# Linear attention with ReLU features: the first octet's K in one transfer or in two

## The chip, the cores and the metric

The kernel runs on one core of a Trainium2 chip. The core has five engines that matter here: TensorE (PE in the profile, with its weight loads as PEld), VectorE (DVE), ScalarE (ACT), GpSimd (POOL) and SyncE (SP). Data moves between the device memory and the on-chip memory (SBUF) through 16 DMA engines, which all queues share. The metric is the device time of one execution in microseconds, the median of several runs.

## The reference

Inputs Q, K and V have the shape (8, 12, 512, 64) in float32: 96 heads of 512 positions with 64 values each. For each head:

```python
Q_feat = np.maximum(0, Q)
K_feat = np.maximum(0, K)
KV = np.einsum('bhkd,bhkv->bhdv', K_feat, V)
K_sum = np.sum(K_feat, axis=2)
numerator = np.einsum('bhqd,bhdv->bhqv', Q_feat, KV)
denominator = np.einsum('bhqd,bhd->bhq', Q_feat, K_sum)
return numerator / (denominator[:, :, :, None] + 1e-10)
```

Each of the three inputs and the output has 12.58 MB, and every byte of them is moved once.

## The kernel before

**Tiling.** The 96 heads are worked on as 12 octets of 8 heads. One octet of one tensor is 1 MB of float32: 128 partitions with 2048 values (8 KB) each. A partition holds 32 consecutive positions ("rows" in the kernel, RQ = 32) of one head, so 16 partitions make up a head. A half of a partition's row is 16 positions (R = 16), 4 KB.

**Loads.** All loads of octets 1 to 11, and of Q for octet 0, are issued by GpSimd and turn float32 into bfloat16 on the way (`load`, line 171). Octets 0 and 1 are loaded one at a time, later ones two octets per transfer (`load_two`, line 177). The input tiles have six places (NI = 6), and the loads use six semaphore lanes in turn, so a load waits until the load six before it has landed. K and V of octet 0 take another way: SyncE loads them as float32 (line 259) into the first two of the ten output tiles, `o_sb[0]` and `o_sb[1]`, which are not needed for output until octets 8 and 9. SyncE's transfers use three lanes in turn (`lanes`, line 156); its first stores go on in the same turn.

**One octet's work.** For octet i, `step(i)` and the TensorE program (`products`, line 350) do this:

- VectorE makes `kf` from K (`prep_k`, line 182: ReLU and a mask by head, in two slots s), ScalarE and VectorE make `vo` from V (`prep_v`, line 189), and VectorE copies Q (`copy_q`, line 199).
- TensorE transposes Q into `ps_qt` (line 360), ScalarE evacuates it with ReLU (`relu_q`, line 203).
- TensorE accumulates K^T V and the sums of K into `ps_kv` (line 369); the products of the first 16 rows wait for the semaphores a0 and d0, those of the other 16 for d1. ScalarE copies the result to `kvd` (`evac_kv`, line 209).
- TensorE forms the denominators and the numerators (line 354), VectorE takes the reciprocals (line 223), the numerators are copied (line 218) and transposed back (line 378), and VectorE multiplies them into the output tile in two halves j (`norm`, line 234).
- SyncE stores the output tile (`store`, line 241). All stores also wait for the last K load (the key `("k", (NO - 1) % NI)`), so that they come behind the loads.

**What sets the order.** The order of instructions on each engine is written out by hand in `body`, `setup` and `step`. The class `Order` turns keys that an instruction reads and writes into semaphore waits: an instruction waits for the last writer of each key that it reads, and for the writer and the readers of each key that it writes. Before, K and V of octet 0 have one key each, `("o", 0)` and `("o", 1)`. In `setup` (line 287) `prep_k(0, 0)` and `prep_k(0, 1)` each take all 32 rows of K, and then follow the three preparations of V. The halves of the output tiles have keys `("o", i, j)`; for the two tiles that held octet 0's K and V, `norm` also writes the common key `("o", i)`.

Of the kernel before, what the change touches and what calls it, by code (L numbers as in the profile page):

```python
# [96 lines left out]
def kernel(  # L97
# [8 lines left out]
    B, H, S, D = Q.shape  # L106
# [5 lines left out]
    R = S * 4 // P  # L112
# [4 lines left out]
    NI = 6  # L117
# [11 lines left out]
    def view(X, f):  # L129
        return X.rearrange("b h s d -> (b h s d)").rearrange("(n p f) -> n p f", p=P, f=f)  # L130

    Qr, Kr, Vr, Or = [view(X, RQ * D) for X in (Q, K, V, out)]
# [3 lines left out]
    mask = sb.tile([P, 2, 2], fp32, name="mask")  # L136
    mask_h = sb.tile([P, 8, 2], fp32, name="mask_h")
    kf = sb.tile([P, RQ, 2, D], bf16, name="kf")
    vo = sb.tile([P, RQ, 2, D4], bf16, name="vo")
# [7 lines left out]
    rec = sb.tile([P, RQ], fp32, name="rec")  # L147
    ins = {n: sb.tile([P, NI, RQ * D], bf16, name=f"{n}_sb") for n in "qkv"}
    o_sb = [sb.tile([P, RQ, D], fp32, name=f"o_sb{i}") for i in range(NOUT)]
# [10 lines left out]
    def lane(who):  # L160
        turn[who] += 1
        return lanes[who][(turn[who] - 1) % len(lanes[who])]

    do = Order(nc, sems)

    def kv_src(o):
        if o == 0:
            return (o_sb[0], ("o", 0)), (o_sb[1], ("o", 1))
        return [(ins[n][:, o % NI].rearrange("p (r d) -> p r d", d=D), (n, o % NI)) for n in "kv"]

    def load(n, *octets):
        o, i, m = octets[0], octets[0] % NI, len(octets)
        src = {"q": Qr, "k": Kr, "v": Vr}[n][o:o + m].rearrange("n p f -> p n f")
        do.op("pool", lambda e: e.dma_start(out=ins[n][:, i:i + m], in_=src, single_packet=True),  # L174
              writes=[(n, x % NI) for x in octets], dma=lane("pool"))

    def load_two(o):
        load("q", o, o + 1)
        load("k", o, o + 1)
        load("v", o, o + 1)  # L180

    def prep_k(o, s, halves=(0, 1)):
        src, key = kv_src(o)[0]
        rs = slice(R * halves[0], R * halves[-1] + R)
        do.op("dve", lambda e: e.tensor_scalar(kf[:, rs, s, :], src[:, rs], scalar1=0.0, scalar2=mask[:, 0, s:s + 1],  # L185
                                               op0=Alu.max, op1=Alu.mult),
              reads=[key, ("mask", 0)], writes=[("kf", s, j) for j in halves])

    def prep_v(o, t, halves, who, sem=None):
        src, key = kv_src(o)[1]  # L190
        rs = slice(R * halves[0], R * halves[-1] + R)
        to, src, m = vo[:, rs, t, 2:D + 2], src[:, rs], mask[:, 1, t:t + 1]
        if who == "act":
            make = lambda e: e.activation(to, src, Act.Copy, scale=m)  # L194
        else:
            make = lambda e: e.tensor_scalar(to, src, scalar1=m, scalar2=None, op0=Alu.mult)  # L196
        do.op(who, make, reads=[key, ("mask", 1), "vo1"], writes=[("vo", t, j) for j in halves], sem=sem)

    def copy_q(o):
        do.op("dve", lambda e: e.tensor_copy(q2.rearrange("p u f -> p (u f)"), ins["q"][:, o % NI]),  # L200
# [33 lines left out]
    def norm(o, j):  # L234
        i = (o + 2) % NOUT
        rs = slice(16 * j, 16 * j + 16)
        do.op("dve", lambda e: e.tensor_tensor(o_sb[i][:, rs], ps_x[j].rearrange("p (r d) -> p r d", d=D),  # L237
                                               rec[:, rs].unsqueeze(2).to_broadcast([P, 16, D]), op=Alu.mult),
              reads=[("x", j), "rec"], writes=[("o", i, j)] if i > 1 else [("o", i, j), ("o", i)], sem=f"n{j}")

    def store(o):
        i = (o + 2) % NOUT
# [11 lines left out]
    def memset(who, ap, value, key):  # L254
        do.op(who, lambda e: e.memset(ap, value), writes=[key] if isinstance(key, (str, tuple)) else key)  # L255

    def body():
        for c, X in enumerate((Kr, Vr)):
            do.op("sp", lambda e: e.dma_start(out=o_sb[c].rearrange("p r d -> p (r d)"), in_=X[0]),
                  writes=[("o", c)], dma=lane("sp"))  # L260
        load("q", 0)
        memset("pool", ident, 0.0, "ident")
        do.op("pool", lambda e: e.affine_select(out=ident, in_=ident, compare_op=Alu.not_equal, fill=1.0, base=0,
                                                pattern=[[-1, P]], channel_multiplier=1),
              reads=["ident"], writes=["ident"])
        for n in "kqv":
            load(n, 1)
        ones = vo[:, :, :, 1:D4 - 1]
        for c in range(4):
            memset("pool", ones[:, 8 * c:8 * c + 8, :, 0:D + 2:D1], 0.0, "vo1")  # L270
        for h in range(4):
            for c in range(4):
                memset("pool", ones[32 * h:32 * h + 32, 8 * c:8 * c + 8, h % 2, 0:D + 2:D1], 1.0, "vo1")
        for h in range(4):
            for t in range(2):
                memset("pool", mask[32 * h:32 * h + 32, 1, t:t + 1], 1.0 if h % 2 == t else 0.0,
                       [("m", h, t), ("mask", 1)])
        setup()
        load_two(2)
        load_two(4)  # L280
        for o in range(NO + 1):
            step(o)
        for n in lanes["pool"] + lanes["sp"]:
            nc.gpsimd.wait_ge(sems[n], do.count[n])
        nc.gpsimd.drain()

    def setup():
        do.op("dve", lambda e: e.tensor_copy(ident32, ident), reads=["ident"], writes=["ident32"])
        for c in range(2):
            do.op("dve", lambda e: e.tensor_reduce(  # L290
                out=mask_h[:, :, c], in_=ident32.rearrange("p (h b) -> p h b", h=8), op=Alu.add,
                axis=mybir.AxisListType.X), reads=["ident32"], writes=[("mh", c), "mask_h"])
        do.op("dve", lambda e: e.tensor_reduce(
            out=mask[:, 0, :], in_=mask_h[:, :, 0].rearrange("p (a s) -> p s a", s=2), op=Alu.add,
            axis=mybir.AxisListType.X), reads=["mask_h"], writes=[("mask", 0)])
        prep_k(0, 0)
        prep_k(0, 1)
        prep_v(0, 1, (0,), "act", "a0")
        prep_v(0, 0, (0, 1), "dve", "d0")
        prep_v(0, 1, (1,), "dve", "d1")  # L300
        do.op("dve", lambda e: e.memset(kvf.bitcast(fp32)[:, 0:4 * D1], 0.0), writes=KVD, sem="n0")
        do.op("dve", lambda e: e.memset(kvf.bitcast(fp32)[:, 4 * D1:], 0.0), writes=KVD, sem="n1")
        copy_q(0)
        for j in range(2):
            nc.scalar.sem_inc(sems[f"t{j}"], 1)
            do.note("act", "act", (), (), f"t{j}", 1)

    def step(i):
        r = i + 1
        more, last = i + 1 < NO, i == NO  # L310

        if not last:
            do.looped([("q2", r)], ["q2", "ident"], [("pq", 0)])
            do.looped([], ["q2", "ident"], [("pq", 1)])
            relu_q(0)
            relu_q(1)
            do.looped([("a0", r), ("d0", r)], KF[0], PK + ["pd"])
            do.looped([("d1", r)], KF[1], PK + ["pd"])
            evac_kv()
            if more:  # L320
                prep_v(i + 1, 1, (0,), "act", "a0")
                copy_q(i + 1)
                for j in range(2):
                    prep_k(i + 1, 0, (j,))
                    prep_k(i + 1, 1, (j,))
        if i > 0:
            o = i - 1
            do.looped([("t0", r), ("t1", r)], [*OT, "ident32"], [("x", 0)])
            do.looped([], [*OT, "ident32"], [("x", 1)])
            for j in range(2):  # L330
                norm(o, j)
            if i % 2 and i + 6 < NO:
                load_two(i + 5)
                if i + 7 == NO:
                    for x in range(o):
                        store(x)
            if i + 7 >= NO:
                store(o)
        if not last:
            do.looped([("ev", r)], [*QT, *KVD], ["pd"])  # L340
            denominators()
            for j in range(2):
                do.looped([(f"n{j}", r)], [*QT, *KVD], [("x", j)])
            copy_ot(0, "act")
            copy_ot(1, "act" if more else "dve")
            if more:
                prep_v(i + 1, 0, (0, 1), "dve", "d0")
                prep_v(i + 1, 1, (1,), "dve", "d1")
# [48 lines left out]
    with tc.tile_critical(no_gpsimd_drain=True):  # L397
        body()
        products()
# [34 lines left out]
```

## Time and profile before

| | us |
|---|---|
| median of 3 runs | 125.28 |
| lowest and highest run | 125.17 and 125.55 |
| the profiled execution | 125.0 |
| its span, from the first instruction to the last | 123.2 |

| engine | busy us | share of the span |
|---|---|---|
| VectorE | 86.8 | 70% |
| TensorE products | 83.2 | 68% |
| ScalarE | 76.6 | 62% |
| TensorE weight loads | 71.6 | 58% |
| GpSimd | 20.3 | 17% |

The profile's page divides the span into 40 slices and gives the busy share of each engine and of the DMA engines in tenths for each slice (9 is 90% or more). The bytes of a DMA are counted as they are written, so a load that turns float32 into bfloat16 counts half of what it reads. A timeline row gives the start, the time taken, the engine, the line, the operation, output and inputs, shapes and count, and in brackets the idle time of the engine before it with what ended it. A "q" behind an engine's name is its sequencer, which issues DMAs. A DMA's landing is when its completion signal has come from all 16 DMA engines.

### The profile page before, as it was taken

How to read it: one execution, taken by the hardware profiler on the slowest of the kernel's cores; microseconds unless marked ns; L12 is line 12 of the kernel's file. 1: busy time of each engine (PE TensorE's matmuls, PEld its weight loads, DVE VectorE, ACT ScalarE, POOL GpSimd, SP SyncE). 2: the span in 40 equal slices, each digit the busy share in tenths (PEclk: the TensorE clock that was granted, in tenths of full speed). 3: DMA queues.
4: the chain of work that ended last, by engine and by line, in shares of the span. 5: the costliest groups of instructions: out<-in, count | busy, mean ns of one | idle time of the engine just before them, and what ended most of it. 6: DMA issues, size and time to landing. Idle time of an engine off the chain costs nothing.

```text
span 123.2 us, 3416 instructions
## 1 busy us (share of the span) xinstructions
PE 83.2 (68%) x1440; PEld 71.6 (58%) x1440; DVE 86.8 (70%) x149; ACT 76.6 (62%) x108; POOL 20.3 (17%) x53
## 2 busy tenths in 40 slices
PE   0000085893498898989979899797996959929100
PEld 0000074793297695977958689595885948819000
DVE  0252936625969989899898989989899794593400
ACT  0000755991099994999949997799945999630000
POOL 5887922012022021020220000000000000000000
PEclk9999999999779999999999999999999999995955
DMA  2999999999999999999999999999999999999991
GB/s 61 396 311 237 213 213 217 217 214 215 214 213 213 214 215 213 214 213 214 215 215 214 219 214 213 215 213 213 214 309 424 426 428 423 423 426 426 426 431 64
DMA packets 6676, 32.55 MB, mean 264 GB/s; under 512 B 528, under 2 KB 528, under 8 KB 4880
## 3 DMA queue, kind: packets, MB, share of 16 engines
q0 software_dynamic: 4656, 17.83, 71.9%
q1 hardware_dynamic: 2016, 14.68, 28.7%
q14 instruction: 3, 0.02, 0.0%
q8 instruction: 1, 0.02, 0.0%
HBM read 37.75 MB, written 12.58 MB: 409 GB/s over the span
## 4 chain that ended last, share of the span: by engine, by line
DMA 64%; POOL 9%; DVE 6%; PE 6%; ACT 5%; issue 3%; POOLq 0%; DVEq 0%; SPq 0%
DMA v_sb<-in_V_dram 64%; POOL vo L255 5%; PE ps_x L378 4%; DVE o_sb L237 3%; PE ps_kv L369 2%; ACT ot_sb L220 2%; ACT qt L204 1%; POOL q_sb L174 1%; POOL k_sb L174 1%; ACT kvd L212 1%; ACT vo L194 1%; DVE ot_sb L220 1%; DVE den L229 1%; POOL mask L255 1%; DVE own L225 1%
## 5 line engine op out<-in xcount | busy, mean ns | idle before, releaser
L237 DVE TENSOR_TENSOR o_sb<-ps_x,rec 128x1024 f32<-128x1024 f32 x24 | 28.5, 1220 | 6.8 <-PE ps_x L378 5.5
L378 PE MATMUL ps_x<-ident,ot_sb 128*128 128x128 f32 x192 | 25.2, 288 | 1.7 <-DVE ot_sb L220 1.7
L369 PE MATMUL ps_kv<-vo,kf 64*128 64x132 bf16 x768 | 25.3, 221 | 1.1 <-DVE vo L196 0.5
L360 PE MATMUL ps_qt<-ident,q 128*128 128x128 bf16 x192 | 14.4, 235 | 16.8 <-DVE q L200 15.9
L369 PEld LDWEIGHTS ps_kv<-vo,kf 64*128 64x128 bf16 x768 | 23.4, 95 | 3.0 <-issue 2.6
L185 DVE TENSOR_SCALAR kf<-k_sb,mask 128x1024 bf16<-128x1024 bf16 x44 | 19.5, 490 | 7.9 <-PE ps_kv L369 3.9
L204 ACT ACTIVATE qt<-ps_qt 128x1024 bf16<-128x1024 bf16 x24 | 23.5, 1040 | 2.1 <-PE ps_qt L360 2.1
L378 PEld LDWEIGHTS ps_x<-ident,ot_sb 128*128 128x128 f32 x192 | 22.3, 148 | 3.2 <-issue 2.0
L360 PEld LDWEIGHTS ps_qt<-ident,q 128*128 128x128 bf16 x192 | 12.5, 106 | 19.2 <-DVE q L200 15.9
L220 ACT COPY ot_sb<-ps_x 128x1024 f32<-128x1024 f32 x23 | 22.2, 1016 | 1.7 <-PE ps_x L354 1.4
L194 ACT ACTIVATE vo<-v_sb,mask 128x1024 bf16<-128x1024 bf16 x11 | 12.7, 1153 | 13.8 <-DMA v_sb<-in_V_dram 13.6
L212 ACT CAST kvd<-ps_kv 64x260 bf16<-64x260 f32 x48 | 18.0, 375 | 2.6 <-PE ps_kv L369 1.6
L354 PE MATMUL ps_x<-qt,kvd 128*128 128x256 bf16 x96 | 14.7, 280 | 6.6 <-DVE o_sb L237 6.2
L354 PEld LDWEIGHTS ps_x<-qt,kvd 128*128 128x128 bf16 x96 | 7.8, 100 | 10.7 <-DVE o_sb L237 9.4
L196 DVE TENSOR_SCALAR vo<-v_sb,mask 128x2048 bf16<-128x2048 bf16 (+1 forms) x22 | 11.6, 568 | 0.0
L200 DVE COPY q<-q_sb 128x2048 bf16<-128x2048 bf16 x12 | 8.6, 716 | 2.7 <-PE ps_qt L360 2.7
L354 PE MATMUL ps_kv<-kvd,qt 128*128 128x16 bf16 x192 | 7.0, 179 | 5.0 <-ACT kvd L212 5.0
L354 PEld LDWEIGHTS ps_kv<-kvd,qt 128*128 128x128 bf16 x192 | 6.1, 96 | 6.5 <-ACT kvd L212 6.3
L194 ACT ACT_TABLE_LOAD x1 | 1.3, 1283 | 12.4 <-DMA o_sb<-in_V_dram 12.4
L174 POOL DMA_DIRECT2D k_sb<-in_K_dram x6 | 4.8, 796 | 14.2 <-DMA k_sb<-in_K_dram 12.6
L174 POOL DMA_DIRECT2D q_sb<-in_Q_dram x7 | 4.7, 678 | 13.6 <-DVE kf L185 8.3
L174 POOL DMA_DIRECT2D v_sb<-in_V_dram x6 | 4.1, 690 | 14.2 <-DMA v_sb<-in_V_dram 14.2
(20 smaller groups left out, 29.6 us busy)
## 6 DMA issues: line engine op xcount, KB each, us to landing
out_dram<-o_sb SPq DMA_DIRECT2D x12, 1024.0 KB, 14.3
q_sb<-in_Q_dram POOLq DMA_DIRECT2D x5, 1024.0 KB, 29.0
k_sb<-in_K_dram POOLq DMA_DIRECT2D x5, 1024.0 KB, 29.0
v_sb<-in_V_dram POOLq DMA_DIRECT2D x5, 1024.0 KB, 29.1
o_sb<-in_K_dram SPq DMA_DIRECT2D x1, 1024.0 KB, 6.5
o_sb<-in_V_dram SPq DMA_DIRECT2D x1, 1024.0 KB, 10.9
q_sb<-in_Q_dram POOLq DMA_DIRECT2D x2, 512.0 KB, 11.5
k_sb<-in_K_dram POOLq DMA_DIRECT2D x1, 512.0 KB, 11.5
```

What stands on the lines that cost most here:

```text
L174: do.op("pool", lambda e: e.dma_start(out=ins[n][:, i:i + m], in_=src, single_packet=True), writes=[(n, x % NI) for x in octets], dma=lane ...
L185: do.op("dve", lambda e: e.tensor_scalar(kf[:, rs, s, :], src[:, rs], scalar1=0.0, scalar2=mask[:, 0, s:s + 1], op0=Alu.max, op1=Alu.mult) ...
L194: make = lambda e: e.activation(to, src, Act.Copy, scale=m)
L196: make = lambda e: e.tensor_scalar(to, src, scalar1=m, scalar2=None, op0=Alu.mult)
L204: do.op("act", lambda e: e.activation(qt[:, j * (U // 2):(j + 1) * (U // 2)], ps_qt[j], Act.Relu), reads=[("pq", j)], writes=[("qt", j)])
L212: do.op("act", lambda e: e.copy(kvd[64 * c:64 * c + 64, s:8:2, c * D1:c * D1 + D1].rearrange("p (g t) d -> p g t d", t=2), ps_kv[64 * s:64 ...
L220: do.op(who, lambda e: e.copy(to, src) if who == "act" else e.tensor_copy(to, src), reads=[("x", j)], writes=[("ot", j)], sem=f"t{j}")
L237: do.op("dve", lambda e: e.tensor_tensor(o_sb[i][:, rs], ps_x[j].rearrange("p (r d) -> p r d", d=D), rec[:, rs].unsqueeze(2).to_broadcast( ...
L354: return pe.matmul(out_, lhsT, rhs, start=True, stop=True, skip_group_check=True)
L360: x = pe.transpose(ps_qt[u // 8][:, u % 8, :], q2[:, u, :], ident)
L369: x = pe.matmul(ps_kv[:, h, 0:2 * (D + 2)].rearrange("p (t d) -> p t d", t=2), kf[ps, R * g + k, :, :].rearrange("p s d -> p (s d)"), vo[p ...
L378: x = pe.transpose(ps_x[u // 8][:, u % 8 * P:u % 8 * P + P], ot[:, u].rearrange("p h c -> p (h c)"), ident32)
```

## The change

K of octet 0 is loaded by SyncE in two transfers, both from all 128 partitions: the first 4 KB of each 8 KB row, then the second 4 KB. V follows as the third transfer, in one piece as before. Each transfer takes the next of SyncE's three lanes. The keys of the two tiles now go by halves, `("o", c, j)`: the transfer of a half writes that half's key, V's transfer writes both. `prep_k` and `prep_v` read the keys of the halves that they take; since both `prep_k` calls for octet 0 still take all 32 rows, they wait for both transfers. `norm` writes the key of its half alone, for all output tiles.

```diff
-    def kv_src(o):
+    def kv_src(o, c, halves):
         if o == 0:
-            return (o_sb[0], ("o", 0)), (o_sb[1], ("o", 1))
-        return [(ins[n][:, o % NI].rearrange("p (r d) -> p r d", d=D), (n, o % NI)) for n in "kv"]
+            return o_sb[c], [("o", c, j) for j in halves]
+        return ins["kv"[c]][:, o % NI].rearrange("p (r d) -> p r d", d=D), [("kv"[c], o % NI)]
...
     def prep_k(o, s, halves=(0, 1)):
-        src, key = kv_src(o)[0]
+        src, keys = kv_src(o, 0, halves)
...
-              reads=[key, ("mask", 0)], writes=[("kf", s, j) for j in halves])
+              reads=[*keys, ("mask", 0)], writes=[("kf", s, j) for j in halves])
...
     def prep_v(o, t, halves, who, sem=None):
-        src, key = kv_src(o)[1]
+        src, keys = kv_src(o, 1, halves)
...
-        do.op(who, make, reads=[key, ("mask", 1), "vo1"], writes=[("vo", t, j) for j in halves], sem=sem)
+        do.op(who, make, reads=[*keys, ("mask", 1), "vo1"], writes=[("vo", t, j) for j in halves], sem=sem)
...
-              reads=[("x", j), "rec"], writes=[("o", i, j)] if i > 1 else [("o", i, j), ("o", i)], sem=f"n{j}")
+              reads=[("x", j), "rec"], writes=[("o", i, j)], sem=f"n{j}")
...
-        for c, X in enumerate((Kr, Vr)):
-            do.op("sp", lambda e: e.dma_start(out=o_sb[c].rearrange("p r d -> p (r d)"), in_=X[0]),
-                  writes=[("o", c)], dma=lane("sp"))
+        for c, X, halves in ((0, Kr, (0,)), (0, Kr, (1,)), (1, Vr, (0, 1))):
+            rs = slice(R * halves[0], R * halves[-1] + R)
+            do.op("sp", lambda e: e.dma_start(out=o_sb[c][:, rs].rearrange("p r d -> p (r d)"),
+                                              in_=X[0][:, rs.start * D:rs.stop * D]),
+                  writes=[("o", c, j) for j in halves], dma=lane("sp"))
```

## The prediction

> **What bounds the kernel now.** I read the page first: the busy tenths by slice, then the chain that ended last (64% of it is one long DMA entry), then the waits of SyncE, then stages of the span, and only then single rows of the timeline around the first octet and the end.
>
> The page's slices say that the DMA engines are full almost from the first slice to the last, while no other engine is.
>
> ```profile
> span 123.2 us, 3416 instructions
> PE   0000085893498898989979899797996959929100
> DVE  0252936625969989899898989989899794593400
> DMA  2999999999999999999999999999999999999991
> HBM read 37.75 MB, written 12.58 MB: 409 GB/s over the span
> ```
>
> Cut into stages (each row: the stage, its length, busy time of PE, PEld, DVE, ACT and POOL, granted clock, DMA share, GB/s), the same is sharper:
>
> ```profile
> 1.00:3.00 2.00, 0.00 (x0) 0.00 (x0) 0.23 (x1) 0.00 (x0) 1.46 (x4) 1.00 0.37 78
> 3.00:5.50 2.50, 0.00 (x0) 0.00 (x0) 0.74 (x3) 0.00 (x0) 2.27 (x8) 1.00 1.01 419
> 34.00:63.00 29.00, 26.62 (x477) 22.86 (x474) 26.07 (x46) 25.21 (x36) 4.29 (x6) 0.97 1.06 214
> 118.00:120.00 2.00, 0.00 (x0) 0.00 (x0) 0.00 (x0) 0.00 (x0) 0.00 (x0) 0.50 1.02 430
> 121.00:123.20 2.20, 0.00 (x0) 0.00 (x0) 0.00 (x0) 0.00 (x0) 0.00 (x0) 0.50 0.04 15
> ```
>
> From 3 us to 120 us the share is 1.01 or above. The 214 GB/s in the middle counts bf16 as written; those loads read twice that from f32, about 428 GB/s, the same rate as the stores. So 50.33 MB at 430 GB/s is 117.0 us, and the flow runs from about 2.7 to about 120.6, with the slowest DMA engine ending near 121.7. The kernel's time is when the flow starts, plus its bytes, plus a short end.
>
> The compute engines don't set the end. The last store is issued at 115.74, and SyncE then waits 5.6 us for it, behind stores already queued. Before that, compute is itself held by the loads at each pair of octets:
>
> ```profile
> SPq L405 <- DMA out_dram<-o_sb: 5.6, 1, 5.6
> ```
> ```profile
> 33.80 1.15 ACT L194 ACTIVATE vo<-v_sb,mask 128x1024 bf16<-128x1024 bf16 x1 [5.60 <-DMA v_sb<-in_V_dram]
> 77.86 1.15 ACT L194 ACTIVATE vo<-v_sb,mask 128x1024 bf16<-128x1024 bf16 x1 [1.62 <-DMA v_sb<-in_V_dram]
> 93.88 1.15 ACT L194 ACTIVATE vo<-v_sb,mask 128x1024 bf16<-128x1024 bf16 x1 [2.88 <-DMA v_sb<-in_V_dram]
> ```
>
> **The change part by part.** All against the profiled execution, 125.0 us (span 123.2 and 1.8 around it); that lies 0.28 below the median of 125.28, and I add the sum to the median.
>
> *Issue on SyncE.* The two transfers of before:
>
> ```profile
> 0.96 0.39 SPq L259 DMA_DIRECT2D o_sb<-in_K_dram  x1
> 1.40 0.43 SPq L259 DMA_DIRECT2D o_sb<-in_V_dram  x1
> 7.53 2.48 DVE L185 TENSOR_SCALAR kf<-o_sb,mask 128x2048 bf16<-128x2048 f32 x2 [3.70 <-DMA o_sb<-in_K_dram]
> 12.44 1.95 DVE L196 TENSOR_SCALAR vo<-o_sb,mask 128x2048 bf16<-128x2048 f32 x2 [2.43 <-DMA o_sb<-in_V_dram]
> ```
>
> One more issue of about 0.43 puts K's second half at 1.40 and V at 1.84 instead of 1.40. The DMA engines have K to do until about 5.2, and V's first packets need about 1 us from issue (K: issued 0.96, only three packets started before 2.0), so V is ready near 2.9 and the delay costs nothing. SyncE's next instruction is a store at 87.68; nothing else is queued behind.
>
> *Between K's halves.* The first half is 512 KB, 1.2 us at 430 GB/s, so it lasts until 3.9 at least; the second half's packets are ready at about 2.4 by the same lead. 1.5 us of cover: no gap, 0. Without cover it would be a gap of up to the lead, 1.0 us.
>
> *Twice the completions.* GpSimd's loads are each released by a landing. Those of one octet (1 MB) are 2.45 us apart, those of two octets (2 MB) 4.87:
>
> ```profile
> 16.93 0.70 POOL L174 DMA_DIRECT2D k_sb<-in_K_dram  x1 [1.64 <-DMA q_sb<-in_Q_dram]
> 19.38 0.71 POOL L174 DMA_DIRECT2D v_sb<-in_V_dram  x1 [1.75 <-DMA v_sb<-in_V_dram]
> 24.33 0.70 POOL L174 DMA_DIRECT2D q_sb<-in_Q_dram  x1 [4.25 <-DMA q_sb<-in_Q_dram]
> 29.20 0.84 POOL L174 DMA_DIRECT2D k_sb<-in_K_dram  x1 [4.17 <-DMA k_sb<-in_K_dram]
> 34.07 0.77 POOL L174 DMA_DIRECT2D v_sb<-in_V_dram  x1 [4.03 <-DMA v_sb<-in_V_dram]
> ```
>
> Two times 2.45 less 4.87 is 0.03: in a queue that is never empty, cutting the same bytes into two transfers costs at most 0.03 us.
>
> *Half-size packets.* K goes from 128 packets of 8 KB to 256 of 4 KB, 8 more on each DMA engine, all on the bounding resource. No row shows a 4 KB read, so I bound it. From 6 to 9 us the two queues share the engines:
>
> ```profile
> q0 software_dynamic: 78, 0.32, 52.3%
> q1 hardware_dynamic: 78, 0.63, 52.2%
> ```
>
> The 4 KB written by the one took 0.523 x 48 / 78 = 0.322 us, the 8 KB of the other 0.321. Since the first kind reads 8 KB too, this fits a price by bytes read (nothing extra), but also a price by packet: then each added packet costs a full one, 8 x 0.306 (2.45 us for 8 rows) = 2.45 us, the upper end. A third row is nearer. Between 5.0 and 5.5 us SyncE's queue has 33 packets, 78.7% of 8 us = 6.30 us, and 13 of them are the few bytes of a completion; the other 20 at 0.309 make 6.18, so a tiny packet takes 0.009 us. That is the part that doesn't go with bytes, and it speaks for the price by bytes: 8 x 0.009 + 0.009 for the added completion = 0.08 us. I take 0.08, which holds the 0.03 above, and keep 0 and 2.45 as ends. Below 0 only an earlier start of the flow could bring it (a rival).
>
> Here the Trainium skill has a figure. Its page "DMA: Bandwidth & Descriptors", section "iDMA fabric — 4 AXI ports for 8 engines, asymmetric across TPBs", gives 408.7 GB/s for a stream of 1 MiB loads from SyncE with 4 KiB rows; by it K's 1.05 MB would take 2.57 us instead of 2.44, and the sum would be +0.13 instead of +0.08. No run here shows such rows yet.
>
> *Waits and turns.* The K preparation on VectorE still takes all 32 rows, so it waits for both halves: one more wait, on an engine that sits idle 3.70 us there anyway. Of the 16 DMA engines, 15 had finished K by 5.5 us (the small packets: 2 before 5.0, 13 after); the last, held by one 16 KB instruction fetch of 0.93 us, finished about 7. There the queues take packets in turn, so with the packets halved K gets one turn more behind a software packet: K and V on that engine land some 0.32 us later, K near 7.8, V near 12.7. VectorE has 2.43 idle between them; the shift of the first products is swallowed by ScalarE's 5.60 at 33.80. Cost 0; uncovered it would be 0.32. SyncE's semaphore lanes move by one, and the stores that reuse lanes of the first loads find them long landed.
>
> *Keys of the output halves.* Normalisations of octets 8 and 9 no longer write the common key, which made the second half wait for the first on VectorE itself: those pairs (90.45 and 98.23) take 2.48 us, pairs such as 83.07 take 2.35. 0.13 twice is saved on VectorE, while SyncE's stores wait in a full queue: 0 at the end.
>
> Sum: +0.08 us on the path, so 125.0 becomes 125.08 and the median 125.28 becomes 125.36 us, +0.06%.
>
> **The rivals.**
>
> *A half packet costs nearly a whole one* (slower). The place is 2.7 to 5.2 us, the price up to 2.45 us: 127.7 us. It decides from 0.047 us per added packet (8 x 0.047 = 0.38, which is 0.3%). For it: reading every second 4 KB is a pattern that no row shows. Against: the 0.009 us of the tiny packets, and the equal price of all 8 KB reads.
>
> *A gap between the halves* (slower). If the second half's packets are made ready only after the first has run, the engines idle for the lead of 1.0 us: 126.4. For it: before 3 us there are only 19 packets, so the start is slow. Against: later transfers follow without a gap (the 0.03). The Trainium skill, same page, section "Anatomy of one DMA — SWDGE (gpsimd) path", gives each DMA a fixed cost of about 2.0 us; paid in series for one more DMA that would be 127.4, but the trace's 2.45 against 4.87 shows no such cost where the queue is full.
>
> *An earlier start of the flow* (faster). If the time from issue to first packet goes with a transfer's bytes, half of 1.04 us is saved: 125.36 - 0.52 = 124.84. It decides from 0.46 us. For it: in the stage from 1 to 3 us the DMA share is only 0.37. Against: the number of rows per transfer, 128, doesn't change.
>
> *Later first products* (slower). V's landing would have to slip by more than the 5.60 at 33.80 before any of it reaches the end; from 0.32 that is far.
>
> **How the numbers follow.** What a measurement of this kernel can tell from no change is about 0.3%, 0.38 us. The forecast, within that, has 0.60. Dearer packets 0.14, a gap 0.08, later products and what I don't see 0.04: slower 0.26. The earlier start 0.12 and 0.02 unseen: faster 0.14. The time is the likeliest case's, 125.36; its own range is 125.0 to 125.7 (the runs of before spread over 0.38). Stretched to the near part of the rivals, half of the earlier start below and 0.8 us of dearer packets or gap above, the range is 124.8 to 126.1; what lies past it holds no more than 0.2.
>
> **What would show it.** Right: SyncE's queue has 144 packets more; the stage 3 to 5.5 us keeps a share near 1 and 419 GB/s; the K preparation starts between 7.4 and 8.0; the first q_sb load of two octets released by a landing stays within 0.2 us of 24.33, the last store's landing likewise. Wrong: a lower rate in the stage from 3 to 5.5 (packet price), a share under 1 between 3 and 4 (gap), packets well before 2.0 (earlier start), or an end that moves while the landings up to 93.9 don't (compute after all).

## The result, and the profile after

The changed kernel takes 125.80 us (125.73 to 125.94) against 125.36 us (125.15 to 125.55) before: a ratio of 1.0042 with a 95% interval of 1.0032 to 1.0051. That is 0.44 us slower, just past the 0.38 us (0.3%) that the prediction named as the bound of no change. The time lies in the stated range of 124.8 to 126.1, but in the case "slower", which had a chance of 0.26, and not in the likeliest one, whose own range was 125.0 to 125.7.

The page of the changed kernel: span, DMA slices with their rates, SyncE's queue, and the chain that ended last by engine.

```profile
span 123.9 us, 3415 instructions
DMA  2999999999999999999999999999999999999990
GB/s 73 317 317 272 213 213 218 213 214 213 213 216 214 213 218 214 214 212 213 217 216 213 218 214 214 212 213 216 214 320 428 426 423 426 420 423 434 423 415 32
q1 hardware_dynamic: 2160, 14.68, 28.9%
PE 39%; DVE 28%; DMA 14%; POOL 8%; issue 4%; POOLq 0%; DVEq 0%; SPq 0%
```

The DMA engines are as full as before. SyncE's queue has 2160 packets instead of 2016, 144 more, and the same bytes. The chain now goes mostly through TensorE and VectorE, which looks as if compute had become the bound. It hasn't. The last store is issued earlier than before, and SyncE then waits longer for it, 6.8 us instead of 5.6. Before:

```profile
115.74 0.33 SPq L246 DMA_DIRECT2D out_dram<-o_sb  x1
```

After:

```profile
115.33 0.33 SPq L246 DMA_DIRECT2D out_dram<-o_sb  x1
```
```profile
SPq L407 <- DMA out_dram<-o_sb: 6.8, 1, 6.8
```

The issue time differs from one execution to the next without moving the end: in e1 below, which has the transfers of before and its time, the last store is issued at 114.55 us and SyncE waits 7.1 us. So the DMA flow still sets the end, and it runs later. The stages of the changed kernel (columns as in the prediction: busy times of PE, PEld, DVE, ACT, POOL, then clock, DMA share and GB/s) show where:

```profile
1.00:3.00 2.00, 0.00 (x0) 0.00 (x0) 0.23 (x1) 0.00 (x0) 1.46 (x4) 1.00 0.38 94
3.00:5.50 2.50, 0.00 (x0) 0.00 (x0) 0.74 (x3) 0.00 (x0) 2.27 (x8) 1.00 1.03 338
34.00:63.00 29.00, 26.67 (x458) 23.14 (x459) 25.38 (x48) 25.47 (x36) 5.00 (x6) 0.94 1.06 215
118.00:120.00 2.00, 0.00 (x0) 0.00 (x0) 0.00 (x0) 0.00 (x0) 0.00 (x0) 0.50 1.02 430
121.00:123.90 2.90, 0.00 (x0) 0.00 (x0) 0.00 (x0) 0.00 (x0) 0.00 (x0) 0.50 0.06 25
```

The middle and the end have the rates of before. Only the stage from 3 to 5.5 us fell, from 419 to 338 GB/s, and there the DMA share stayed at 1.03: the engines count as busy while they move less. Packets of GpSimd's queue, which count half of what they read, start a little earlier in this stage than before, so part of the 338 is bookkeeping. The single microseconds before they start are clean. Before:

```profile
2.00:3.00 1.00, 0.00 (x0) 0.00 (x0) 0.23 (x1) 0.00 (x0) 0.93 (x4) 1.00 0.57 131
3.00:4.00 1.00, 0.00 (x0) 0.00 (x0) 0.74 (x3) 0.00 (x0) 1.00 (x3) 1.00 0.99 418
4.00:5.00 1.00, 0.00 (x0) 0.00 (x0) 0.00 (x0) 0.00 (x0) 0.89 (x4) 1.00 1.11 459
```

After:

```profile
2.00:3.00 1.00, 0.00 (x0) 0.00 (x0) 0.23 (x1) 0.00 (x0) 0.93 (x4) 1.00 0.66 176
3.00:4.00 1.00, 0.00 (x0) 0.00 (x0) 0.74 (x3) 0.00 (x0) 1.00 (x3) 1.00 1.02 270
4.00:5.00 1.00, 0.00 (x0) 0.00 (x0) 0.00 (x0) 0.00 (x0) 0.89 (x4) 1.00 1.00 389
```

From 3 to 4 us, while K's first halves are being read, 270 GB/s move instead of 418. The runs below in which SyncE's first transfer has whole 8 KB rows in all 128 partitions (e1, e4, e6, e9, e10) have 393 to 410 there, so this row is clear. The row from 2 to 3 us is not: the same runs have 106 to 172, since a packet counts where it starts and 16 engines with one 8 KB packet each are 131 KB. Over the three rows the changed kernel moved 835 KB, before 1008, those runs 917 to 1020; the 82 to 185 KB that are missing are 0.19 to 0.43 us at 430 GB/s. GpSimd's loads, each released by the landing of an earlier one, show the delay further on. The last of them before, and then five of the changed kernel:

```profile
63.49 0.70 POOL L174 DMA_DIRECT2D v_sb<-in_V_dram  x1 [4.24 <-DMA v_sb<-in_V_dram]
```
```profile
17.81 0.70 POOL L174 DMA_DIRECT2D k_sb<-in_K_dram  x1 [1.75 <-DMA q_sb<-in_Q_dram]
20.32 0.73 POOL L174 DMA_DIRECT2D v_sb<-in_V_dram  x1 [1.81 <-DMA v_sb<-in_V_dram]
25.20 0.80 POOL L174 DMA_DIRECT2D q_sb<-in_Q_dram  x1 [4.15 <-DMA q_sb<-in_Q_dram]
30.07 0.71 POOL L174 DMA_DIRECT2D k_sb<-in_K_dram  x1 [4.07 <-DMA k_sb<-in_K_dram]
64.36 0.70 POOL L174 DMA_DIRECT2D v_sb<-in_V_dram  x1 [3.90 <-DMA v_sb<-in_V_dram]
```

Against the rows of before (16.93, 19.38, 24.33, 29.20, and 63.49 for the last) they are 0.88, 0.94, 0.87, 0.87 and 0.87 late. Against the same rows of e1 (17.05, 19.51, 24.46, 29.33, 63.62) it is 0.74 to 0.81. This is more than the 0.44 of the medians: a landing waits for the slowest of the 16 DMA engines, and single executions differ. The span grew by 0.7; of that, 0.3 is that the profiled execution of before lay 0.36 below its median and this one (125.73) only 0.07 below.

That the loss is made at the start and never grows is shown better by bytes. The packets of a trace can be added up in order of their ends, with those of GpSimd's queue counted twice, since it reads twice what it writes. By this count the changed kernel is 0.21 us ahead of before at 0.1 MB, 0.21 behind at 0.5 MB, when K's first half is in, 0.38 behind at 1 MB, and from there 0.31 to 0.43 behind up to 50 MB. Against e1 it is 0.35 ahead, 0.09 behind, 0.24 behind and then 0.22 to 0.33 behind. (That it is ahead at 0.1 MB is in part that a 4 KB packet ends sooner than one of 8 KB.) So the loss is made while K is read, and nothing later adds to it.

The first octet's rows, from the timelines of SyncE and VectorE:

```profile
0.96 0.86 SPq L260 DMA_DIRECT2D o_sb<-in_K_dram  x2
1.87 0.42 SPq L260 DMA_DIRECT2D o_sb<-in_V_dram  x1
8.43 2.48 DVE L185 TENSOR_SCALAR kf<-o_sb,mask 128x2048 bf16<-128x2048 f32 x2 [4.60 <-DMA o_sb<-in_K_dram]
```

The K preparation starts at 8.43 instead of 7.53. On ScalarE the shift is swallowed where the prediction said: its wait for V of octet 2, at 34.69, shrank from 5.60 to 3.77 us and did not vanish.

```profile
34.69 1.16 ACT L194 ACTIVATE vo<-v_sb,mask 128x1024 bf16<-128x1024 bf16 x1 [3.77 <-DMA v_sb<-in_V_dram]
94.76 1.16 ACT L194 ACTIVATE vo<-v_sb,mask 128x1024 bf16<-128x1024 bf16 x1 [2.10 <-DMA v_sb<-in_V_dram]
```

### The profile page after: what moved, and what is told of

The parts are those of the page before. It is cut to its first block, busy times and chain, and to the rows that moved or that the text cites. A ratio compares the mean times of both kernels' runs of the same rounds, so it can differ in the third digit from the quotient of the medians.

```text
span 123.9 us, 3415 instructions
## 1 busy us (share of the span) xinstructions
PE 84.4 (68%) x1440; PEld 73.1 (59%) x1440; DVE 86.3 (70%) x149; ACT 77.2 (62%) x108; POOL 21.2 (17%) x53
## 3 DMA queue, kind: packets, MB, share of 16 engines
q1 hardware_dynamic: 2160, 14.68, 28.9%
## 4 chain that ended last, share of the span: by engine, by line
PE 39%; DVE 28%; DMA 14%; POOL 8%; issue 4%; POOLq 0%; DVEq 0%; SPq 0%
DVE o_sb L237 23%; PE ps_kv L371 17%; DMA k_sb<-in_K_dram 14%; PE ps_x L380 9%; PE ps_qt L362 8%; PE ps_x L356 4%; POOL vo L255 4%; DVE kf L185 2%; POOL q_sb L174 1%; POOL mask L255 1%; DVE ot_sb L220 1%; DVE den L229 1%; DVE own L225 1%; DVE rec L232 1%; DVE vo L196 0%
## 5 line engine op out<-in xcount | busy, mean ns | idle before, releaser
L371 PE MATMUL ps_kv<-vo,kf 64*128 64x132 bf16 x768 | 27.3, 231 | 0.6
L362 PE MATMUL ps_qt<-ident,q 128*128 128x128 bf16 x192 | 15.2, 242 | 17.5 <-DVE q L200 16.6
L371 PEld LDWEIGHTS ps_kv<-vo,kf 64*128 64x128 bf16 x768 | 25.4, 100 | 2.5 <-issue 2.5
L362 PEld LDWEIGHTS ps_qt<-ident,q 128*128 128x128 bf16 x192 | 13.1, 110 | 20.3 <-DVE q L200 16.6
L380 PE MATMUL ps_x<-ident,ot_sb 128*128 128x128 f32 x192 | 23.6, 276 | 1.7 <-DVE ot_sb L220 1.7
L380 PEld LDWEIGHTS ps_x<-ident,ot_sb 128*128 128x128 f32 x192 | 20.8, 140 | 3.2 <-issue 2.0
L194 ACT ACTIVATE vo<-v_sb,mask 128x1024 bf16<-128x1024 bf16 x11 | 12.7, 1154 | 8.9 <-DMA v_sb<-in_V_dram 8.7
L174 POOL DMA_DIRECT2D v_sb<-in_V_dram x6 | 5.1, 850 | 13.8 <-DMA v_sb<-in_V_dram 13.8
L174 POOL DMA_DIRECT2D k_sb<-in_K_dram x6 | 4.6, 765 | 14.2 <-DMA k_sb<-in_K_dram 12.5
```

Source lines behind the costliest of these rows:

```text
L362: x = pe.transpose(ps_qt[u // 8][:, u % 8, :], q2[:, u, :], ident)
L371: x = pe.matmul(ps_kv[:, h, 0:2 * (D + 2)].rearrange("p (t d) -> p t d", t=2), kf[ps, R * g + k, :, :].rearrange("p s d -> p (s d)"), vo[p ...
L380: x = pe.transpose(ps_x[u // 8][:, u % 8 * P:u % 8 * P + P], ot[:, u].rearrange("p h c -> p (h c)"), ident32)
```

## The experiments

All diffs are against the changed kernel. "Row" below is one partition's piece in a transfer. The times at a glance:

| run | SyncE's transfers of octet 0 | us | before, same chip | ratio (95%) |
|---|---|---|---|---|
| changed | K halves, V | 125.80 | 125.36 | 1.0042 (1.0032 to 1.0051) |
| e1 | K, V; new keys | 125.29 | 125.30 | 0.9999 (0.9990 to 1.0008) |
| e2 | V, K halves | 126.07 | 125.30 | 1.0064 (1.0050 to 1.0078) |
| e3 | K as 256 pieces in one, V | 125.68 | 125.30 | 1.0031 (1.0020 to 1.0043) |
| e4 | K, V halves | 125.91 | 125.30 | 1.0055 (1.0041 to 1.0068) |
| e5 | K in contiguous halves, V | 125.07 | 125.38 | 0.9979 (0.9970 to 0.9988) |
| e6 | K, V in contiguous halves | 125.46 | 125.38 | 1.0008 (1.0000 to 1.0017) |
| e7 | K by even and odd partitions, V | 125.71 | 125.38 | 1.0032 (1.0022 to 1.0043) |
| e8 | K; V from ScalarE's queue | 125.44 | 125.38 | 1.0003 (0.9994 to 1.0012) |
| e9 | K, V second halves, V first halves | 125.81 | 125.33 | 1.0035 (1.0022 to 1.0048) |
| e10 | K, V first halves, another octet's second halves | 125.93 | 125.33 | 1.0049 (1.0032 to 1.0066) |
| e11 | K by lower and upper 64 partitions, V | 126.71 | 125.33 | 1.0111 (1.0094 to 1.0128) |
| e12 | K quarters, V | 126.45 | 125.33 | 1.0095 (1.0069 to 1.0122) |

The first theory (S) was that SyncE's queue hands rows to the engines at a limited pace, too slow for small ones; its rivals were a price per small packet (P) and a price per further transfer (B).

**e1, the keys alone.**

```diff
-        for c, X, halves in ((0, Kr, (0,)), (0, Kr, (1,)), (1, Vr, (0, 1))):
+        for c, X, halves in ((0, Kr, (0, 1)), (1, Vr, (0, 1))):
```

> The changed kernel with K in one transfer again; only the keys by halves and their waits stay changed. Theory S (supply): SyncE's queue hands rows to the DMA engines at a limited pace, about 66 rows a microsecond in the stage 3 to 4 us of the changed kernel (270 GB/s of 4 KB rows), and 4 KB rows are drained faster than that, so the engines starve at the start. Theory P (packet price): each added 4 KB packet costs about 0.055 us on its engine (0.44 / 8) wherever it lies. Theory B (boundary): each further transfer in SyncE's queue costs about 0.4 us. All three expect the time of before, 125.36 (125.2 to 125.5), and 418 GB/s from 3 to 4 us. A fourth, that the keys and waits cost the time, expects 125.8.

Measured 125.29 against 125.30. The keys and waits cost nothing and gain nothing; the split is the cause.

**e2, V first, then K's halves.**

```diff
+        for c, X, halves in ((1, Vr, (0, 1)), (0, Kr, (0,)), (0, Kr, (1,))):
```

> The changed kernel with V (8 KB rows) issued first and K's two halves behind it. S: V's rows carry 0.55 MB per us at the same pace, enough for the engines, and K's rows are made ready while V runs: about 125.4 (125.2 to 125.55), 400 GB/s or more from 3 to 4 us. P: 125.8, as many 4 KB packets. B: 125.8, as many transfers. The later K preparation (some 3 us) is expected to be swallowed by ScalarE's wait for V of octet 2 in all three.

Measured 126.07, 0.64% slower, worse than the change itself. S was wrong here: V's rows went at 393 GB/s from 3 to 4 us, near the 400 that it gave, but the loss came all the same, later, when K's halves ran beside GpSimd's queue (the "software queue" from here on, q0 in the profile): from 6 to 9 us 166 packets of both queues started, 217 GB/s, and each software packet took 0.399 us (66.5% of 48 us, which is 3 us of 16 engines, over 80 packets).

**e3, one transfer of 256 pieces of 4 KB.** The second halves go into the third output tile, so that the pieces can't be joined; taken together the transfer reads the whole 1 MB in order.

```diff
+    k_in = o_all[:, 0:4:2, 0:R, :]
...
+        do.op("sp", lambda e: e.dma_start(out=k_in.rearrange("p h r d -> p h (r d)"),
+                                          in_=Kr[0].rearrange("p (h f) -> p h f", h=2)),
+              writes=[("o", 0, 0), ("o", 2, 0)], dma=lane("sp"))
```

> K in a single transfer, but with 4 KB rows: the second halves go to the first half of the third output tile, so that the 256 pieces can't be joined. S: the slow start stays, 125.6 to 125.95, and 250 to 300 GB/s from 3 to 4 us. P: 125.8. B: 125.36, since there is one transfer.

Measured 125.68, in the range that S gave, but not for its reason:

```profile
2.00:3.00 1.00, 0.00 (x0) 0.00 (x0) 0.23 (x1) 0.00 (x0) 0.93 (x4) 1.00 0.51 33
3.00:4.00 1.00, 0.00 (x0) 0.00 (x0) 0.74 (x3) 0.00 (x0) 1.00 (x3) 1.00 0.85 319
4.00:5.00 1.00, 0.00 (x0) 0.00 (x0) 0.00 (x0) 0.00 (x0) 0.89 (x4) 1.00 0.99 401
```

The flow starts later (33 KB from 2 to 3 us, against 106 to 172 with 128 whole rows; its first packet starts at 2.39 us, against 1.99 before), and then 4 KB pieces reach 401 GB/s. Counted in bytes, it is 0.44 us behind before at 0.1 MB and 0.48 at 5 MB. So the one transfer of twice as many rows lost time by a later start; that is another loss than the change's, where the first packet starts at 1.98 and the bytes after it are slow.

**e4, V in halves instead of K.**

```diff
+        for c, X, halves in ((0, Kr, (0, 1)), (1, Vr, (0,)), (1, Vr, (1,))):
```

> K whole (8 KB rows), V in two transfers of 4 KB rows. S: K's rows cover the making of V's; the software queue is there when V's rows fall short, so nothing or little is lost: 125.3 to 125.55, 418 GB/s from 3 to 4 us. P: 125.8. B: 125.8.

Measured 125.91: S fell a second time. From 6 to 9 us, where V's first halves run beside the software queue (q0), and from 10 to 12.5, where the second halves do:

```profile
DMA packets 163, 0.64 MB, mean 214 GB/s; under 512 B 7, under 2 KB 7, under 8 KB 162
...
q0 software_dynamic: 82, 0.34, 71.7%
q1 hardware_dynamic: 81, 0.31, 29.0%
DMA packets 189, 0.71 MB, mean 285 GB/s; under 512 B 15, under 2 KB 15, under 8 KB 189
```

A software packet takes 0.717 x 48 / 82 = 0.420 us in the first window, against 0.322 before. So not only V's halves but also the loads beside them are slowed. The other packets of the first window took (0.290 x 48 - 0.06) / 74 = 0.187 us. That left two theories: the pattern that is read (H), every second 4 KB of device memory, called striped below; and turns between the queues with short packets (T). The next two runs change only which 4 KB pieces a transfer reads.

**e5, K in two transfers, each of a contiguous half.**

```diff
-                                              in_=X[0][:, rs.start * D:rs.stop * D]),
+                                              in_=X[0] if len(halves) == 2 else
+                                              X[0][64 * halves[0]:64 * halves[0] + 64].rearrange("p (y f) -> (p y) f", y=2)),
```

> The changed kernel, but each of K's two transfers reads one contiguous half of octet 0's 1 MB as 128 pieces of 4 KB, instead of every second 4 KB. The writes into SBUF, the sizes, the rows and the transfers stay; K of octet 0 lands in the wrong places, so the first octet's output isn't the reference's. Theory H (pattern read): reading only every second 4 KB of device memory is slow (270 GB/s against 418 from 3 to 4 us), and slows the software queue's loads beside it too; it expects the loss to vanish, 125.2 to 125.45, with 390 GB/s or more from 3 to 4 us. Theory S (supply of rows by SyncE's queue) and every theory that goes by packet size or by the writes expect 125.65 to 125.9 and 270 to 300 GB/s.

Measured 125.07, which is 0.21% (0.12 to 0.30) faster than before, and 0.13 us below the range that H gave. This decides the main question. From 3.2 to 4.8 us, the changed kernel:

```profile
DMA packets 139, 0.52 MB, mean 323 GB/s; under 512 B 16, under 2 KB 16, under 8 KB 138
...
q1 hardware_dynamic: 138, 0.50, 94.3%
```

and e5:

```profile
DMA packets 183, 0.68 MB, mean 425 GB/s; under 512 B 20, under 2 KB 20, under 8 KB 182
...
q1 hardware_dynamic: 178, 0.65, 100.8%
```

With tiny packets at 0.009 us taken out, a 4 KB packet took (0.943 x 25.6 - 0.14) / 122 = 0.197 us in the changed kernel and (1.008 x 25.6 - 0.18) / 158 = 0.162 us in e5. Same size, same count, same places in SBUF, same two transfers; only every second 4 KB became consecutive 4 KB. The 0.197 is a mean of two rates. From 3.2 to 4.0 us, in K's first half, a 4 KB packet of the changed kernel took 0.248 us and one of e5 0.161; from 4.2 to 4.8 us, in the second half, the changed kernel's took 0.161 too. Only the first striped transfer is slow. e5's flow also moves more in its first microsecond:

```profile
2.00:3.00 1.00, 0.00 (x0) 0.00 (x0) 0.23 (x1) 0.00 (x0) 0.92 (x4) 1.00 0.86 270
3.00:4.00 1.00, 0.00 (x0) 0.00 (x0) 0.74 (x3) 0.00 (x0) 1.00 (x3) 1.00 1.06 422
```

270 KB from 2 to 3 us instead of 106 to 172; the 98 to 164 KB more are 0.23 to 0.38 us at 430 GB/s, and 0.31 was gained. Its first packet starts no earlier (2.02 us, against 1.98 in the changed kernel and 1.99 before). It is no kernel to keep as it stands, since K lands in the wrong places; a layout that reads so and lands rightly was not tried.

**e6, V in two contiguous halves.** The edit of e5 on e4.

> The run with V in two transfers, but each of the two reads a contiguous half of octet 0's V as 128 pieces of 4 KB; V of octet 0 lands in the wrong places, so the first octet's output isn't the reference's. There the software queue's packets took 0.420 us each from 6 to 9 us (71.7% of 48 us over 82) instead of 0.322. H: they take 0.32 again and the time is 125.2 to 125.45. Theory T (turns: a packet of the one queue behind a short packet of the other is not fetched in time): they stay at 0.40 to 0.44 and the time at 125.8 to 126.0.

Measured 125.46, the same as before but for 0.17% at most, and 0.01 past the range that H gave. The two windows of e4 again:

```profile
DMA packets 211, 0.80 MB, mean 266 GB/s; under 512 B 16, under 2 KB 16, under 8 KB 211
...
q0 software_dynamic: 106, 0.43, 71.2%
q1 hardware_dynamic: 105, 0.36, 32.6%
DMA packets 183, 0.68 MB, mean 270 GB/s; under 512 B 18, under 2 KB 18, under 8 KB 183
```

A software packet takes 0.712 x 48 / 106 = 0.322 us and one of V's pieces (0.326 x 48 - 0.14) / 89 = 0.174. T is out: here short packets in turns cost nothing when the pieces are consecutive.

**e7, K by even and odd partitions, 8 KB rows.**

```diff
+        for x in range(2):
+            do.op("sp", lambda e: e.dma_start(out=o_sb[0][x::2].rearrange("p r d -> p (r d)"), in_=Kr[0][x::2]),
+                  writes=[("o", 0, x)], dma=lane("sp"))
```

> K in two transfers of 8 KB rows, the even partitions and the odd ones, so 64 rows each; nothing is read by halves. H, S and T: no slow rows, 125.36 or a little less: with one transfer of 256 rows the flow started some 0.45 us later than with 128, so with 64 it may start 0.2 earlier, 125.1 to 125.35. B (each further transfer costs about 0.4): 125.7.

Measured 125.71, as B said and against the others. But its stages show another loss: 66 KB from 2 to 3 us instead of 106 to 172, and then 393 GB/s from 3 to 4. SyncE also took longer to issue the two, 1.19 us against 0.86 in the changed kernel. The flow started later: its first packet starts at 2.32 us, and counted in bytes it is 0.30 us behind before at 0.1 MB and 0.36 at 5 MB. (The row from 4 to 5 us reads only 258 GB/s, but software packets run in it already, and they count half.) e5 and e6, which have as many transfers and no such loss, exclude a fixed price of 0.4 us per transfer.

**e8, V from ScalarE's queue.** K whole from SyncE, V whole from ScalarE, on a lane of its own, at the same time.

> K whole from SyncE as before, V whole from ScalarE's own queue, issued at the same time as K. If the start of the flow (DMA share 0.37 from 1 to 3 us) is held by one queue's making of rows, two queues fill it sooner: up to 0.35 us less, 124.95 to 125.3. If the start is held by something that both queues share, 125.3 to 125.45. V's landing comes earlier or equal in both.

Measured 125.44, no change (0.9994 to 1.0012). Two queues gave 164 KB from 2 to 3 us, no more than single queues gave, and then only 287 GB/s from 3 to 4. So a second queue did not fill the start sooner.

**e9, V's second halves first.** H had two readings: the second 4 KB of each 8 are quick because of where they lie (H1), or because the stretch has been visited (H2).

```diff
+        for c, X, halves in ((0, Kr, (0, 1)), (1, Vr, (1,)), (1, Vr, (0,))):
```

> K whole, V in two transfers of every second 4 KB, but the second halves of the rows first. In the run with the first halves first, only the first of the two transfers was slow: 163 packets of all queues from 6 to 9 us (211 with contiguous halves), 189 from 10 to 12.5 (183 with contiguous halves). Theory H2 (a first visit by halves is slow, the second visit to the same stretch of memory is not): again 155 to 175 packets from 6 to 9 and 180 to 195 from 10 to 12.5, time 125.8 to 126.05. Theory H1 (reading the first 4 KB of 8 is slow, the second 4 KB not): about 205 from 6 to 9 and 140 to 155 from 10 to 12.5.

Measured 125.81, and again the transfer that comes first is the slow one (179 packets in the first window, a little above the range that H2 gave, 183 in the second; with contiguous halves 211 and 183):

```profile
DMA packets 179, 0.70 MB, mean 233 GB/s; under 512 B 9, under 2 KB 9, under 8 KB 178
...
q0 software_dynamic: 89, 0.36, 61.4%
q1 hardware_dynamic: 90, 0.34, 39.6%
DMA packets 183, 0.71 MB, mean 285 GB/s; under 512 B 9, under 2 KB 9, under 8 KB 183
```

H1 is out. But here the software packets of the first window took 0.614 x 48 / 89 = 0.331 us, hardly more than in e6, and V's own pieces (0.396 x 48 - 0.08) / 81 = 0.233 instead of 0.174. So which of the two queues shows the loss is not the same in every run.

**e10, the second halves of another octet.**

```diff
-                                              in_=X[0][:, rs.start * D:rs.stop * D]),
+                                              in_=X[halves == (1,)][:, rs.start * D:rs.stop * D]),
```

> K whole, then the first halves of the rows of V's octet 0, then the second halves of the rows of V's octet 1, 1 MB further on (so half of octet 0's V is another octet's, and the first octet's output isn't the reference's). H2: the second transfer now is a first visit too and as slow as the first: 155 to 175 packets from 6 to 9 us and 140 to 160 from 10 to 12.5, time 126.2 to 126.6. If only the first such transfer of an execution is slow, or only first halves: 180 to 195 from 10 to 12.5, 125.8 to 126.05.

Measured 125.93, with 178 and 187 packets:

```profile
DMA packets 178, 0.69 MB, mean 231 GB/s; under 512 B 9, under 2 KB 9, under 8 KB 178
...
DMA packets 187, 0.70 MB, mean 282 GB/s; under 512 B 15, under 2 KB 15, under 8 KB 187
```

The second transfer reads a stretch that nothing has visited (GpSimd's own load of it starts after 15 us), and is not slow. H2 is out too. What is left is what was seen: in the changed kernel (270, then 389 GB/s) and in e2, e4, e9 and e10, the first striped transfer is slow and the second is not. From 10 to 12.5 us a software packet takes 0.322 us in e2, e4, e6, e9 and e10 alike, and a 4 KB piece 0.170 to 0.172. Why only the first stays open.

**e11, K by lower and upper 64 partitions, 8 KB rows, each transfer contiguous.**

```diff
+        for x in range(2):
+            do.op("sp", lambda e: e.dma_start(out=o_sb[0][64 * x:64 * x + 64].rearrange("p r d -> p (r d)"),
+                                              in_=Kr[0][64 * x:64 * x + 64]),
+                  writes=[("o", 0, x)], dma=lane("sp"))
```

> K in two transfers of 64 partitions each with whole 8 KB rows, so each transfer reads a contiguous 512 KB, and the output is the reference's. Pattern theories (H): nothing is slow, 125.0 to 125.4; the lower end if a transfer of half the bytes starts the flow earlier, as in the run with contiguous halves (270 GB/s from 2 to 3 us against 131 before), the upper end if the split by partitions starts it later, as with even and odd partitions (66). Theory B: 125.7.

Measured 126.71, outside every expectation. From 3.2 to 4.8 us:

```profile
DMA packets 59, 0.37 MB, mean 230 GB/s; under 512 B 10, under 2 KB 10, under 8 KB 20
...
q1 hardware_dynamic: 48, 0.31, 87.0%
```

Of the 48 packets 38 are 8 KB (0.31 MB): (0.870 x 25.6 - 0.09) / 38 = 0.58 us each, nearly twice the 0.309 of before. What e11 has alone is that one transfer writes 64 neighbouring partitions: e5 read the same contiguous 512 KB, and e7 had transfers of 64 whole rows, both without slow packets. The Trainium skill's page "DMA: Bandwidth & Descriptors", section "Rules for kernel authors", advises against two transfers to the two halves of the partitions because they serialize. The advice holds here, but the trace shows more than no gain: while one half of the partitions takes all writes, a packet takes nearly twice as long.

**e12, K in quarters of 2 KB.**

SyncE's lanes are five instead of three here, one for each transfer.

```diff
+        for x in range(4):
+            do.op("sp", lambda e: e.dma_start(out=o_sb[0][:, 8 * x:8 * x + 8].rearrange("p r d -> p (r d)"),
+                                              in_=Kr[0][:, 8 * x * D:(8 * x + 8) * D]),
+                  writes=[("o", 0, x // 2, x % 2)], dma=lane("sp"))
```

> K in four transfers, each of one 2 KB quarter of every 8 KB row. H2: the first quarter reads 0.26 MB at 135 GB/s or less instead of 0.6 us at full rate, some 1.3 us more, of which 0.4 show in the changed kernel already for halves; the later quarters run at full rate: 126.1 to 126.8. If each quarter is slow: 127.5 or more. If the price is one for the twice-as-many packets (0.055 us each): 126.7 too, but then without a slow stage, the loss spread evenly over 2.5 to 5.5 us.

Measured 126.45, in the range that H2 gave (written before e10 was known) and near the 126.7 of a packet price; the stage decides between the two:

```profile
2.00:3.00 1.00, 0.00 (x0) 0.00 (x0) 0.23 (x1) 0.00 (x0) 0.92 (x4) 1.00 0.63 186
3.00:4.00 1.00, 0.00 (x0) 0.00 (x0) 0.74 (x3) 0.00 (x0) 1.00 (x3) 1.00 0.63 143
4.00:5.00 1.00, 0.00 (x0) 0.00 (x0) 0.00 (x0) 0.00 (x0) 0.89 (x4) 1.00 0.91 203
```

It starts no later than the halves (186 KB from 2 to 3 us) and then moves 143 and 203 GB/s, where halves moved 270 and 389 and whole rows 418 and 459. The thinner the slice of each 8 KB, the slower. By transfer, a 2 KB packet took 0.117 and 0.127 us in the first two and 0.096 and 0.095 in the last two, so the loss is early here as well, but not in the first transfer alone. The share of 0.63 there says that the engines also stood empty, so at 2 KB the making of rows (four transfers of 128) may add its part; this run can't separate the two.

## Why the prediction was right and wrong

*What bounds the kernel* was right. Every run that lost time lost it early in the DMA flow and kept the loss to the end. This is how far each flow, counted in bytes, lies behind the trace of before, in us, when 5 MB have been moved (at about 15 us) and when 48 MB have (about 115 us):

| run | changed | e2 | e3 | e4 | e7 | e9 | e10 | e11 | e12 | e1 (no loss) | e6 (no loss) | e8 (no loss) |
|---|---|---|---|---|---|---|---|---|---|---|---|---|
| at 5 MB | 0.36 | 0.77 | 0.48 | 0.90 | 0.36 | 0.79 | 0.71 | 1.43 | 1.35 | 0.11 | 0.12 | 0.17 |
| at 48 MB | 0.34 | 0.88 | 0.49 | 0.92 | 0.41 | 0.82 | 0.78 | 1.50 | 1.37 | 0.09 | 0.19 | 0.18 |

Compute moved without effect, even where the last store was issued earlier (0.4 us in the changed kernel, 1.2 in e1).

*Issue on SyncE and the completions* were right: 0.86 and 0.42 us of issue are hidden, and e5 and e6, each with one transfer more, show no price of it beyond 0.17% (the upper end in e6). *The keys* were right at 0 (e1); the pairs at 92.12 and 99.50 take 2.36 us, 0.12 less than before, and nothing follows from it.

*Between K's halves* was right: no gap opens (DMA share 1.02 from 3 to 4 us, 1.00 from 4 to 5). The 419 GB/s that the last part of the prediction expected to stay did not, but for the reason of the next step.

*Half-size packets* is the step that failed. It weighed a price by bytes against a price by packet, took 0.08, and kept 2.45 as the far end. For consecutive pieces the price by bytes is right: 0.162 us for 4 KB in e5, about half of the 0.309 for 8 KB. But the packets of K's halves were not only smaller, they also left out every second 4 KB, and so they cost (1.02 x 16) / 66 = 0.247 us from 3 to 4 us (270 KB are 66 packets), and 0.161 only in the second transfer. Where the sum had 0.08 us, the kernel shows 0.44.

The mechanism that came true is the rival "a half packet costs nearly a whole one", in the place that it named, with the reason that it gave ("reading every second 4 KB is a pattern that no row shows"), but at 0.44 us instead of up to 2.45. Its threshold of 0.047 us per added packet fits: 0.44 / 8 is 0.055. But it is not a price of each added packet, as that rival had it, since the second transfer's packets and e5's cost nothing extra. The sign named for a packet price came, a lower rate from 3 to 5.5 us, and two signs of "right" failed: the K preparation starts at 8.43 instead of between 7.4 and 8.0, and the q_sb load of two octets is released at 25.20 instead of within 0.2 of 24.33. That the stated range holds 125.80 is owed to the 0.8 us kept for the rivals, not to the sum. The forecast should have given more weight to that rival: the evidence against it, the 0.009 us of tiny packets and the equal price of 8 KB reads, came from rows that were all consecutive.

The Trainium skill's figure for 4 KiB rows (page "DMA: Bandwidth & Descriptors", section "iDMA fabric — 4 AXI ports for 8 engines, asymmetric across TPBs"), by which the sum was +0.13 us, was nearer than the 0.08 and still a third of what was measured. In the trace of e5 consecutive 4 KB rows reach 422 GB/s from 3 to 4 us, no less than the page's 408.7.

*Waits and turns* was right in direction and short in size: the K preparation came 0.90 us later and not 0.32, V's 13.33 instead of 12.7. The runs don't tell how much of this is the further turn that the prediction counted and how much the slower pieces. The cover held, as 5.60 became 3.77.

*The gap between the halves* and *later first products* did not come. *The earlier start* can't be told in the changed kernel, whose 176 KB from 2 to 3 us lie next to the 106 to 172 of whole rows. In e5, with 270, there is a gain: counted in bytes it is 0.25 us ahead of before at 5 MB, and the kernel was 0.21% faster. But the reason that the rival gave, a time to the first packet that goes with a transfer's bytes, is not it: with half the bytes the first packet starts at 1.98 us (changed kernel) and 2.02 (e5), against 1.99 before.

## What to carry to other kernels

When a transfer is cut, look at the addresses that each part reads, not only at its size: halves made by cutting every row read memory in stripes, halves made of consecutive pieces don't, and here that alone was the difference between 0.42% slower and 0.21% faster. In a kernel bound by its DMA flow, as this one, the first few microseconds count in full: what was lost there was still missing at the end. The DMA engines' share read 1.02 while the rate was a third lower, so read GB/s beside the share. A chain of work that turns to compute isn't proof: the last store's issue time and the wait for it tell which side sets the end.

## What the runs showed of the hardware that was not expected

- Striped reads can slow others too: beside V's first halves the software queue's packets took 0.420 us instead of 0.322 (e4), beside consecutive pieces 0.322 (e6). In e9 they took 0.331, and the striped pieces themselves 0.233 instead of 0.174. With halves, only the first striped transfer of an execution was slow, whichever half it took (e9) and wherever the second went (e10). Whether this sits in the device memory or in how SyncE's rows are made is open; e5 and e6 change both by the same edit.
- The Trainium skill, page "DMA: Bandwidth & Descriptors", section "Latency and other measured facts", reports slow copies at row pitches of 512 KiB and more, and infers that partitions' streams fall on the same memory channels. Here it is 4 KB pieces at a pitch of 8 KB that are slow (270 against 418 GB/s), while 8 KB pieces at 16 KB are not (e7, 393 from 3 to 4 us). No run here can show channels, and the second striped transfers, at full rate with the same pitch, speak against the pitch alone.
- The start differed with the shape of the first transfer: from 2 to 3 us it moved 106 to 172 KB with 128 whole rows, 33 with 256 pieces, 66 with every second partition, 270 with 128 consecutive pieces of 4 KB. The last three are one execution each.
- While a transfer wrote only 64 neighbouring partitions, packets took nearly twice as long: 0.58 us for 8 KB instead of 0.309 (e11). That the writes are the cause is concluded from e5 and e7, not tested apart.
